# RMSNorm and projection: the rows of a triple loaded as quarters on four partition groups and turned by one VectorE transpose

## The chip, the cores and the metric

The kernel runs on one core of a Trainium2 chip. The metric is device time in microseconds, the median of three runs: 346.23 us for the kernel before (346.22 to 347.12). Engine names follow the profile: PE is TensorE (matmul), PEld its weight load, DVE is VectorE, ACT is ScalarE, POOL is GpSimd, SP is SyncE, which here only issues DMAs.

## The reference

```python
rms = np.sqrt(np.mean(x ** 2, axis=-1, keepdims=True) + eps)
x_norm = x / rms * gamma
return np.matmul(x_norm, w_qkv).astype(np.float32)
```

x is 8 x 1024 x 768 f32 (8192 rows), gamma 768, w_qkv 768 x 2304, the result 8192 x 2304 f32. The kernel needs x twice in different shapes: by rows for the mean of squares, and turned (the 768 inner elements on the partitions) as the left operand of the matmul.

## The kernel before

**Tiling.** The 8192 rows are 64 tiles of 128. The first seven are "plain" (PLAIN = 7): each is cast to bf16, turned by TensorE, multiplied by the bf16 weights `w_b` and scaled by its 1/rms while it leaves PSUM (`cast`, `stat`, `tr`, `cp`, `mm`, `evac`, `store`). They give TensorE work while w is loaded, multiplied by gamma (`conv`), bounded (`bound` to `scales`) and made into f16 operands (`unit`, `bsum`). The other 57 tiles are 19 "triples" of 384 rows. A triple times w is a block product of 3 row tiles x 2 halves of the inner dimension x 3 column thirds, done with 15 block products where the plain way has 18: 11 sums of x blocks (`sum_`, table ASUMS, on POOL, for triple 0 on VectorE too), 15 weight operands (six blocks and eleven combinations share the 15 slots, table BSUMS, made once), and 16 evacuations that combine partial results (`ev`, table VALUES: five plain ones on ACT, eleven with an addition on VectorE). One product (`prod`, matmul at L659) is three blocks of 128 by two column halves of 384: six matmuls. The inner index is split as k = 256 j + 2 m + two: "two" is the half, j = 0 to 2 the block, m the partition of the turned x.

**A triple's way in.** `load_t` (L599) loads 384 rows in one DMA into one of two buffers `xin`: partition p holds rows 3p to 3p+2, 9 KB in one piece. Three `tstat` (L607, ACT Square with an accumulator, 768 elements) give the sums of squares; `trms` (L611, ACT square root, 128x3) and `trecip` (L616, VectorE) make 1/rms. Three `tcast` (L450 through the helper `scaled`) write f16 rows times 1/rms into `xb`. Tile 0 is turned by three f32 TensorE transposes on f16 pairs seen as f32 (`ptr`, L503) and copied out of PSUM by ACT (`pcp`, L442); tiles 1 and 2 by two transposing DMAs from SBUF to SBUF (`pxbar`, L642, "the crossbar"). The turned triple stands in one of four slots of `xT`. `pstore` (L675) stores a third of a tile's columns, nine to a triple.

**The order.** It is written out by hand: the list PLAN names every operation once, and the kernel emits them in that order under `manual_schedule`, so that each engine's own order is that of the list. Each engine works in order, and a wait holds up what stands behind it on the same engine. The DMA queues are in order too: SP issues the loads of w and of the plain tiles, `load_t` 0 and 1, all stores and the crossbar transfers; ACT issues `load_t` 2 to 18 between its own instructions. Buffers: `xin` 2, `xb` 2, `xT` 4, `su` (the sums) 2, seven output buffers `outb`, nine more lent in `w_b` once w has been converted, and the eight PSUM banks in pairs. In the middle of the kernel the list reads, for TensorE, the preparation of x and the loads (evacuations, sums and stores left out):

```python
('prod', 8, 0, 1, 2), ('load_t', 11, 1, 'ACT'), ('trms', 10), ('prod', 8, 1, 1, 0), ('prod', 8, 2, 3, 4),
('prod', 8, 0, 2, 2), ('prod', 8, 1, 2, 0), ('prod', 8, 2, 4, 4), ('trecip', 10), ('tcast', 10, 0, 'p', 0, 'ACT'),
('prod', 8, 0, 3, 2), ('tcast', 10, 1, 'x', 0, 'ACT'), ('ptr', 10, 0, 6, 2), ('prod', 9, 2, 0, 0),
('tcast', 10, 2, 'x', 0, 'ACT'), ('pxbar', 10, 2, 1), ('prod', 9, 3, 0, 4), ('ev', 9, 'h2', 'P', 2)
```

Triple k uses `xin` buffer k mod 2 (the second argument of `load_t`), so `load_t` 11 writes over the rows of triple 9, and in ACT's order it stands behind the statistics of triple 10.

Of the kernel before, what the change touches and what calls it, by code (L numbers as in the profile page):

```python
# [38 lines left out]
    ('stat', 3), ('cp', 0, 'DVE', 1, 3), ('load_w', 9), ('load_w', 8), ('idle', 3, 0), ('tr', 3, 5), ('conv', 3, 3,
    'DVE'), ('prms', 3, 4), ('load_w', 10), ('precip', 3, 4), ('cp', 3, 'ACT'), ('mm', 0, 0, None, '3', 2), ('bound',  # L40
    0, 0, 'DVE'), ('load_x', 4, 4), ('cast', 1, 0, 'POOL', 0, 1), ('load_w', 12), ('stat', 1), ('mm', 3, 0, None, '0',
    6), ('load_w', 13), ('mm', 3, 0, None, '3', 6), ('conv', 4, 4, 'POOL'), ('load_w', 15), ('tr', 1, 0, 0, 1),
    ('cast', 1, 0, 'ACT', 1, 3), ('load_w', 14), ('cp', 1, 'ACT', 0, 1), ('idle', 1, 0), ('tr', 1, 1, 1, 3),
# [37 lines left out]
    None, '4', 0), ('tstat', 0, 2), ('mm', 4, 1, None, '2', 0), ('store', 3, 1), ('bsum', 't10', 1, 'DVE'), ('mm', 4,
    1, None, '3', 0), ('mm', 0, 2, None, '03', 2), ('tstat', 0, 0), ('bsum', 't4', 0, 'DVE'), ('mm', 0, 2, None, '14',
    2), ('bsum', 't5', 0, 'DVE'), ('trms', 0), ('mm', 0, 2, None, '25', 2), ('evac', 6, 1, 4, 'ACT'), ('trecip', 0),
    ('bsum', 't10', 0, 'DVE'), ('mm', 4, 1, None, '1', 0), ('mm', 4, 1, None, '5', 0), ('tcast', 0, 0, 'p', 0, 'ACT'),
    ('store', 6, 1), ('bsum', 't6', 0, 'DVE'), ('mm', 4, 2, None, '03', 4), ('evac', 0, 2, 5, 'ACT'), ('mm', 4, 2,
    None, '14', 4), ('tcast', 0, 1, 'x', 0, 'DVE'), ('mm', 4, 2, None, '25', 4), ('evac', 4, 1, 6, 'DVE'), ('unit',
    'b12', 1, 'ACT'), ('tcast', 0, 2, 'x', 0, 'POOL'), ('store', 0, 2), ('ptr', 0, 0, 2, 0), ('evac', 4, 2, 0, 'DVE'),
    ('mm', 1, 2, None, '03', 0), ('pcp', 0, 0, 'ACT'), ('pxbar', 0, 0, 2), ('mm', 1, 2, None, '14', 0), ('bsum', 't0',
    1, 'DVE'), ('tstat', 1, 1), ('mm', 2, 2, None, '03', 4), ('bsum', 't2', 0, 'DVE'), ('tstat', 1, 0), ('pxbar', 0,
    0, 1), ('mm', 2, 2, None, '25', 4), ('unit', 'b12', 0, 'DVE'), ('mm', 2, 2, None, '14', 4), ('tstat', 1, 2),  # L90
# [633 lines left out]
```

## Time and profile before

| | us |
|---|---|
| median of three runs | 346.23 |
| the profiled execution, its span | 344.0 |
| PE busy | 334.6 (97%) |
| DVE busy | 257.6 (75%) |
| ACT busy | 232.4 (68%) |
| POOL busy | 196.3 (57%) |
| all DMA: 115.61 MB | mean 336 GB/s |

The profile is of one execution. Its span runs from the first to the last instruction that it shows; the time of a run is taken on the device around the whole program and is 2.2 us longer. The parts of the page that are used below: the busy time of each engine; the span in 40 slices; the DMA queues with packets, megabytes and the share of the 16 DMA engines that their packets took; the groups of instructions by line, tile and shape, with count, busy time, mean ns of one, and the idle time of the engine ahead of them with what ended it; and the DMA issues with the median time from issue to landing. Of the trace's views, the windows give, for each stretch, its length and then for PE, PEld, DVE, ACT and POOL the busy us with the number of instructions, then the granted TensorE clock, the busy share of the DMA engines and GB/s; the timeline lists instructions with start, length, engine, line and the wait ahead; the view of one line gives shortest, median and longest ns and the first and the last start.

### The profile page before, as it was taken

How to read it: one execution, taken by the hardware profiler on the slowest of the kernel's cores; microseconds unless marked ns; L12 is line 12 of the kernel's file. 1: busy time of each engine (PE TensorE's matmuls, PEld its weight loads, DVE VectorE, ACT ScalarE, POOL GpSimd, SP SyncE). 2: the span in 40 equal slices, each digit the busy share in tenths (PEclk: the TensorE clock that was granted, in tenths of full speed). 3: DMA queues.
4: the chain of work that ended last, by engine and by line, in shares of the span. 5: the costliest groups of instructions: out<-in, count | busy, mean ns of one | idle time of the engine just before them, and what ended most of it. 6: DMA issues, size and time to landing. Idle time of an engine off the chain costs nothing. (4 is left out here: it accounts for less than half of the span.)

```text
span 344.0 us, 5987 instructions
## 1 busy us (share of the span) xinstructions
PE 334.6 (97%) x2078; PEld 202.2 (59%) x2078; DVE 257.6 (75%) x310; ACT 232.4 (68%) x354; POOL 196.3 (57%) x226
## 2 busy tenths in 40 slices
PE   7889999999999999999999999999999999999994
PEld 2556665666666666666666666666666666666662
DVE  3799999958677685957769595785959668596785
ACT  4589999578665849486684947768494778636310
POOL 1363114579394755929467492947739394891900
PEclk9999999999999999999999999999999999999998
DMA  7999999999999999999999999999999999977848
GB/s 266 402 398 417 404 303 326 309 359 320 321 380 326 392 305 363 305 333 382 286 397 297 361 336 326 395 299 387 302 344 365 318 393 311 374 299 219 339 174 312
DMA packets 64820, 115.61 MB, mean 336 GB/s; under 512 B 34195, under 2 KB 34710, under 8 KB 62358
## 3 DMA queue, kind: packets, MB, share of 16 engines
q1 hardware_dynamic: 62336, 95.18, 82.4%
q10 hardware_dynamic: 2454, 20.06, 18.1%
q8 instruction: 16, 0.26, 0.3%
q14 instruction: 14, 0.11, 0.1%
HBM read 32.25 MB, written 75.50 MB: 313 GB/s over the span
## 5 line engine op out<-in xcount | busy, mean ns | idle before, releaser
L659 PE MATMUL ps<-wq,su 128*128 128x384 f16 x1254 | 213.1, 326 | 0.0
L659 PEld LDWEIGHTS <-su 128*128 128x128 f16 x1254 | 122.7, 98 | 79.3
L455 POOL TENSOR_TENSOR su<-xT 128x384 f16<-128x384 f16 x73 | 64.6, 914 | 92.5 <-DMA xT<-xb 51.3
L672 DVE SCALAR_TENSOR_TENSOR outb<-ps,sc,pp 128x768 f32<-128x768 f32 (+1 forms) x83 | 82.2, 1001 | 18.3 <-PE ps L659 15.8
L659 PE MATMUL ps<-wq,xT 128*128 128x384 f16 x456 | 81.1, 326 | 0.0
L670 ACT ACTIVATE pp<-ps,sc 128x768 f32<-128x768 f32 x76 | 66.8, 904 | 14.4 <-PE ps L659 13.9
L672 DVE SCALAR_TENSOR_TENSOR pp<-ps,sc,pp 128x768 f32<-128x768 f32 x38 | 38.7, 1017 | 40.1 <-PE ps L659 39.9
L450 ACT ACTIVATE xb<-xin,rstd 128x768 f16<-128x768 f32 x53 | 48.7, 974 | 24.2 <-DVE rstd L616 24.1
L659 PEld LDWEIGHTS <-xT 128*128 128x128 f16 x456 | 44.6, 98 | 29.2
L672 DVE SCALAR_TENSOR_TENSOR w_b<-ps,sc,pp 128x768 f32<-128x768 f32 x51 | 51.6, 1015 | 2.3 <-ACT pp L670 0.6
L455 POOL TENSOR_TENSOR su<-su,xT 128x384 f16<-128x384 f16 x56 | 50.5, 925 | 4.7 <-DVE su L455 4.5
L670 ACT ACTIVATE outb<-ps,sc 128x768 f32<-128x768 f32 x19 | 17.1, 898 | 52.8 <-PE ps L659 52.8
L607 ACT ACTIVATE junk<-xin 128x768 bf16<-128x768 f32 x57 | 48.1, 844 | 0.6
L455 POOL TENSOR_TENSOR su<-su 128x384 f16<-128x384 f16 x38 | 35.4, 932 | 3.9 <-DVE su L455 1.0
L531 PE MATMUL ps<-w_b,su 128*128 128x384 bf16 x180 | 31.5, 326 | 1.9 <-DVE w_b L448 1.3
L455 POOL TENSOR_TENSOR su<-xT,su 128x384 f16<-128x384 f16 x36 | 32.3, 914 | 0.2
L531 PEld LDWEIGHTS <-su 128*128 128x128 bf16 x180 | 17.0, 98 | 14.0 <-issue 1.6
L672 DVE SCALAR_TENSOR_TENSOR w_b<-ps,sc,w_b 128x768 f32<-128x768 f32 x17 | 17.3, 1018 | 7.0 <-PE ps L659 5.1
L672 DVE SCALAR_TENSOR_TENSOR pp<-ps,sc,outb 128x768 f32<-128x768 f32 x19 | 19.3, 1016 | 0.6
L455 DVE TENSOR_TENSOR wq<-wq 128x1152 f16<-128x1152 f16 x22 | 18.6, 871 | 0.3
L442 ACT COPY xT<-ps 128x768 f16<-128x768 f16 (+1 forms) x20 | 15.8, 791 | 1.1 <-PE ps L503 1.0
L452 POOL TENSOR_SCALAR w_b<-wq,g_sb 128x768 bf16<-128x768 f32 x9 | 8.1, 905 | 7.9 <-DMA wq<-in_w_qkv_dram 6.6
(59 smaller groups left out, 151.8 us busy)
## 6 DMA issues: line engine op xcount, KB each, us to landing
out_dram<-outb SPq DMA_DIRECT2D x123, 384.0 KB, 6.2
out_dram<-w_b SPq DMA_DIRECT2D x68, 384.0 KB, 5.7
xin<-in_x_dram ACTq DMA_DIRECT2D x17, 1152.0 KB, 7.3
wq<-in_w_qkv_dram SPq DMA_DIRECT2D x14, 384.0 KB, 7.7
xin<-in_x_dram SPq DMA_DIRECT2D x2, 1152.0 KB, 11.9
pp<-in_x_dram SPq DMA_DIRECT2D x5, 384.0 KB, 7.5
wq<-in_w_qkv_dram SPq DMA_DIRECT2D x2, 768.0 KB, 9.2
xT<-xb SPq DMA_TRANSPOSE x38, 5.9
```

The source lines that it names most:

```text
L442: nc.scalar.copy(out=out, in_=in_)
L450: nc.scalar.activation(out=out, in_=in_, func=AF.Copy, scale=scale, bias=0.0)
L452: nc.gpsimd.tensor_scalar(out=out, in0=in_, scalar1=scale, scalar2=1.0, op0=mult, op1=mult)
L455: (nc.vector if eng == "DVE" else nc.gpsimd).tensor_tensor(out=out, in0=a, in1=b, op=op)
L531: nc.tensor.matmul(out=ps[:, b + hh, :CW], lhsT=XT[t][:, two, j, :], rhs=w_b[:, kb, n0:n0 + CW], start=(n == 1), stop=(n == KO), skip_grou ...
L607: nc.scalar.activation(out=junk[:, :K], in_=TX[k][:, i, :], func=AF.Square, accum_out=RS[k][:, i:i + 1])
L659: nc.tensor.matmul(out=ps[:, b + h, :CW], lhsT=left(k, a)[:, j, :], rhs=operand(w)[:, j, CW * h:CW * (h + 1)], start=(i == 0 and j == 0), ...
L670: nc.scalar.activation(out=o, in_=p, func=AF.Copy, scale=SC[sg], bias=0.0)
L672: nc.vector.scalar_tensor_tensor(out=o, in0=p, scalar=SC[sg], in1=q, op0=mult, op1=add if hs > 0 else sub)
```

## The change

x of a triple is loaded in another shape, and turned in another way.

- `load_t` takes the source as `"m (a q) -> a m q"`: partition 32a + r holds quarter a (192 elements, 768 B) of the rows 12r to 12r + 11. Each of a row's four quarters lies on another group of 32 partitions.
- `tstat` therefore has four instructions of 192 elements per tile where it had one of 768, and fills 12 columns of partial sums. A new `tsum` adds the four groups: one f32 matmul on TensorE with the constant `fold4` (128 x 128) and 12 columns, into PSUM. `trms` reads that from PSUM; `trms` and `trecip` work on 128 x 12.
- `tcast` has four instructions of 192 elements per tile.
- A new `tturn` turns a whole triple with one VectorE instruction: 32 x 32 blocks of f16 pairs seen as f32, 128 x 1152, from `xb` into `xT`. Which of the two halves an element belongs to is now the innermost index of `xT`, so the sums and the matmuls that read x itself take every other f16.
- `ptr`, `pcp`, `pxbar` and their helpers are gone: 57 turns on TensorE, 19 copies on ACT and 38 crossbar transfers.
- Since the order of the inner index on the partitions is now another, w is read with it: `"(a j c two) n -> a c j two n"`, and gamma and the partial loads and casts of the first plain tile likewise (`third`).
- PLAN is made anew. The counts of the other operations are the same. In the middle of the kernel it reads, cut as above:

```python
('prod', 8, 0, 1, 2), ('load_t', 11, 1, 'ACT'), ('prod', 8, 1, 1, 0), ('prod', 8, 2, 3, 4), ('prod', 8, 0, 2, 2),
('prod', 8, 1, 2, 0), ('tsum', 10, 6), ('trms', 10), ('prod', 8, 2, 4, 4), ('trecip', 10), ('tcast', 10, 0, 0, 'ACT'),
('prod', 8, 0, 3, 2), ('tcast', 10, 1, 0, 'ACT'), ('prod', 9, 2, 0, 0), ('tcast', 10, 2, 0, 'ACT'),
('tturn', 10, 1), ('prod', 9, 3, 0, 4), ('ev', 9, 'h2', 'P', 2)
```

The diff without PLAN, and without the lines that only drop the removed helpers:

```diff
     ctx.enter_context(tc.manual_schedule())
 
-    g3 = singles.tile([H, 2 * P], f32, name="g3")
-    nc.scalar.dma_start(out=g3, in_=gamma.rearrange("(j q) -> j q", q=2 * P))
+    Q = K // 4
+    g3 = singles.tile([H, 4, Q // H], f32, name="g3")
+    nc.scalar.dma_start(out=g3, in_=gamma.rearrange("(a j q) -> j a q", a=4, j=H))
     eps_sb = singles.tile([P, 1], f32, name="eps_sb")
     nc.vector.memset(eps_sb, float(eps))
...
     ident = singles.tile([P, P], bf16, name="ident")
     nc.vector.tensor_copy(out=ident, in_=ident_f)
-    ident_h = singles.tile([P, P], f16, name="ident_h")
-    nc.vector.tensor_copy(out=ident_h, in_=ident_f)
+    fold4 = singles.tile([P, 4, P // 4], f32, name="fold4")
+    nc.vector.tensor_reduce(out=fold4[:, 0, :], in_=ident_f.rearrange("p (a r) -> p r a", a=4), axis=mybir.AxisListType.X, op=add)
+    for a in range(1, 4):
+        nc.vector.tensor_copy(out=fold4[:, a, :], in_=fold4[:, 0, :])
     ones = singles.tile([1, P], bf16, name="ones")
     nc.gpsimd.memset(ones, 1.0)
...
     wq = singles.tile([P, 15 * H * C], f16, name="wq")
     w_b = singles.tile([P, KO, N], bf16, name="w_b")
-    xin = singles.tile([P, 2, 3, K], f32, name="xin")
+    xin = singles.tile([P, 2, 3 * K], f32, name="xin")
     pp = singles.tile([P, 7, C], f32, name="pp")
     xb = singles.tile([P, 2, 3 * K], f16, name="xb")
...
     zeros = nc.const_aps.tensor(0.0, [P, 1], f32).bitcast(bf16)[:, :1].to_broadcast([P, 512])
     wst = wq.bitcast(f32)
-    wv = w_qkv.rearrange("(j p two) n -> p j two n", p=P, two=2)
+    wv = w_qkv.rearrange("(a j c two) n -> a c j two n", a=4, j=H, two=2)
     lent = w_b.rearrange("p k n -> p (k n)").bitcast(f32)
     xbp = xb.rearrange("p a k -> p (a k)").bitcast(bf16)
...
             nc.tensor.matmul(out=ps[:, b, :], lhsT=zeros[:, :P], rhs=zeros, start=True, stop=True, skip_group_check=True)
 
+    def third(v, a, e):
+        return v.rearrange("p (g j q) -> p g j q", g=4, j=H)[:, :, a:e, :]
+
     def load_x(t, s, a=0, e=H):
         X[t] = pp[:, s, :]
-        nc.sync.dma_start(out=X[t][:, 2 * P * a:2 * P * e], in_=xf[t * P:(t + 1) * P, 2 * P * a:2 * P * e])
+        v = xf[t * P:(t + 1) * P, :]
+        if (a, e) == (0, H):
+            nc.sync.dma_start(out=X[t], in_=v)
+        else:
+            nc.sync.dma_start(out=third(X[t], a, e), in_=third(v, a, e))
 
     def load_w(i):
         twos, j, c, n0, n = PIECES[i]
         n1 = C * c + n0
-        nc.sync.dma_start(out=WF[i], in_=wv[:, j, twos[0]:twos[-1] + 1, n1:n1 + n])
+        nc.sync.dma_start(out=WF[i], in_=wv[:, :, j, twos[0]:twos[-1] + 1, n1:n1 + n])
 
     def gamma_in(b):
...
             two, j = divmod(kb, H)
             if j == 0:
-                nc.tensor.transpose(out=PT["g"][:, kb:kb + H], in_=g3[:, two::2], identity=ident_f[:H, :H])
+                nc.tensor.transpose(out=PT["g"][:, kb:kb + H], in_=g3.rearrange("j a q -> j (a q)")[:, two::2], identity=ident_f[:H, :H])
 
     def gamma_cp():
...
     def cast(t, s, eng, a=0, e=H):
         XB[t] = xbp[:, s * K:(s + 1) * K]
-        copy(eng, XB[t][:, 2 * P * a:2 * P * e], X[t][:, 2 * P * a:2 * P * e])
+        copy(eng, XB[t].rearrange("p (j g q) -> p g j q", g=4, j=H)[:, :, a:e, :], third(X[t], a, e))
 
     def stat(t):
...
 
     def load_t(k, s, eng="SP"):
-        TX[k] = xin[:, s, :, :]
+        TX[k] = xin[:, s, :]
         r0 = base + 3 * P * k
-        (nc.scalar if eng == "ACT" else nc.sync).dma_start(out=TX[k], in_=xf[r0:r0 + 3 * P, :].rearrange("(p i) k -> p i k", i=3))
+        (nc.scalar if eng == "ACT" else nc.sync).dma_start(out=TX[k], in_=xf[r0:r0 + 3 * P, :].rearrange("m (a q) -> a m q", a=4))
+
+    def rows(v, g, i):
+        return v[:, Q * (3 * g + i):Q * (3 * g + i + 1)]
 
     def tstat(k, i):
         if k not in RS:
-            RS[k] = stats.tile([P, 3], f32, name="ssq")
-        nc.scalar.activation(out=junk[:, :K], in_=TX[k][:, i, :], func=AF.Square, accum_out=RS[k][:, i:i + 1])
+            RS[k] = stats.tile([P, 12], f32, name="ssq")
+        for g in range(4):
+            n = 3 * g + i
+            nc.scalar.activation(out=junk[:, Q * (n % 8):Q * (n % 8 + 1)], in_=rows(TX[k], g, i), func=AF.Square, accum_out=RS[k][:, n:n + 1])
+
+    def tsum(k, b):
+        PT[k, "s"] = ps[:, b, :12]
+        nc.tensor.matmul(out=PT[k, "s"], lhsT=fold4.rearrange("p a r -> p (a r)"), rhs=RS[k], start=True, stop=True)
 
     def trms(k):
-        r = stats.tile([P, 3], f32, name="rms")
-        nc.scalar.activation(out=r, in_=RS[k], func=AF.Sqrt, scale=inv_k, bias=eps_sb)
+        r = stats.tile([P, 12], f32, name="rms")
+        nc.scalar.activation(out=r, in_=PT[k, "s"], func=AF.Sqrt, scale=inv_k, bias=eps_sb)
         RS[k] = r
 
     def trecip(k):
-        r = stats.tile([P, 3], f32, name="rstd")
+        r = stats.tile([P, 12], f32, name="rstd")
         nc.vector.reciprocal(out=r, in_=RS[k])
         RS[k] = r
 
-    def tcast(k, i, how, s, eng):
+    def tcast(k, i, s, eng, g0=0, g1=4):
         XBS[k] = s
-        TB[k, i] = xb[:, s, i * K:(i + 1) * K]
-        o, v = TB[k, i], TX[k][:, i, :]
-        if how == "x":
-            o = o.rearrange("p (two j m) -> p two j m", two=2, j=H)
-            v = v.rearrange("p (j m two) -> p two j m", two=2, j=H)
-        scaled(eng, o, v, RS[k][:, i:i + 1])
-
+        for g in range(g0, g1):
+            n = 3 * g + i
+            scaled(eng, rows(xb[:, s, :], g, i), rows(TX[k], g, i), RS[k][:, n:n + 1])
+
+    def tturn(k, s):
+        v = xb[:, XBS[k], :].bitcast(f32).rearrange("p (g b c) -> p g b c", g=4, c=P // 4)
+        o = xT[:, s, :].bitcast(f32).rearrange("p (b r g) -> p g b r", g=4, r=P // 4)
+        nc.vector.transpose(out=o, in_=v)
+        for i in range(3):
+            TT[k, i] = xT[:, s, i * K:(i + 1) * K].rearrange("p (j m two) -> p two j m", two=2, j=H)
 
     def left(k, a):
```

More of the change, by code (lines that the diff above doesn't have):

```diff
@@ L39 @@
[L39 to L43, printed above, removed]
@@ L81 @@
[L81 to L85, printed above, removed]
@@ L86 @@
[L86 to L90, printed above, removed]
@@ new lines @@
+    ('cp', 0, 'DVE', 0, 1), ('load_w', 6), ('idle', 1, 0), ('mm', 0, 0, None, '0', 2), ('cast', 0, 1, 'DVE', 1, 3), ('stat', 0),
+    ('load_w', 2), ('tr', 0, 4, 1, 3), ('load_w', 11), ('load_w', 5), ('cast', 3, 2, 'POOL'), ('stat', 3),
+    ('cp', 0, 'DVE', 1, 3), ('load_w', 9), ('load_w', 8), ('idle', 3, 0), ('tr', 3, 5), ('conv', 3, 3, 'DVE'), ('prms', 3, 4),
+    ('load_w', 10), ('precip', 3, 4), ('cp', 3, 'ACT'), ('mm', 0, 0, None, '3', 2), ('bound', 0, 0, 'DVE'), ('load_x', 4, 4),
+    ('cast', 1, 0, 'POOL', 0, 1), ('load_w', 12), ('stat', 1), ('mm', 3, 0, None, '0', 6), ('load_w', 13),
@@ new lines @@
+    ('mm', 3, 0, None, '3', 6), ('conv', 4, 4, 'POOL'), ('load_w', 15), ('tr', 1, 0, 0, 1), ('cast', 1, 0, 'ACT', 1, 3),
+    ('load_w', 14), ('cp', 1, 'ACT', 0, 1), ('idle', 1, 0), ('tr', 1, 1, 1, 3), ('load_x', 5, 5), ('conv', 1, 1, 'DVE'),
[8 rows of a table added]
+    ('evac', 1, 0, 0, 'DVE'), ('mm', 0, 0, None, '5', 2), ('conv', 8, 2, 'POOL'), ('evac', 0, 0, 1, 'ACT'),
+    ('evac', 2, 0, 2, 'DVE'), ('store', 1, 0), ('mm', 0, 1, None, '0', 4), ('mm', 0, 1, None, '2', 4), ('conv', 10, 4, 'POOL'),
+    ('bound', 1, 0, 'ACT'), ('store', 0, 0), ('mm', 0, 1, None, '5', 4), ('bound', 1, 2, 'DVE'), ('mm', 0, 1, None, '1', 4),
@@ new lines @@
+    ('store', 2, 0), ('mm', 1, 1, None, '0', 2), ('cast', 4, 4, 'POOL'), ('mm', 0, 1, None, '4', 4), ('mm', 1, 1, None, '2', 2),
+    ('bound', 1, 1, 'ACT'), ('tr', 4, 0), ('evac', 3, 0, 3, 'DVE'), ('mm', 1, 1, None, '3', 2), ('mm', 1, 1, None, '4', 2),
+    ('cp', 4, 'DVE'), ('mm', 1, 1, None, '5', 2), ('conv', 12, 0, 'POOL'), ('store', 3, 0), ('stat', 4),
+    ('mm', 1, 1, None, '1', 2), ('mm', 4, 0, None, '0', 6), ('evac', 1, 1, 4, 'DVE'), ('mm', 4, 0, None, '2', 6),
+    ('conv', 12, 3, 'POOL'), ('load_t', 1, 1), ('mm', 4, 0, None, '5', 6), ('prms', 4, 5), ('mm', 4, 0, None, '3', 6),
@@ new lines @@
+    ('precip', 4, 5), ('mm', 4, 0, None, '4', 6), ('bound', 2, 0, 'DVE'), ('store', 1, 1), ('conv', 13, 1, 'ACT'),
+    ('conv', 13, 4, 'POOL'), ('mm', 4, 0, None, '1', 6), ('mm', 0, 1, None, '3', 4), ('mm', 2, 1, None, '0', 0),
+    ('evac', 4, 0, 5, 'ACT'), ('conv', 15, 5, 'POOL'), ('mm', 2, 1, None, '4', 0), ('mm', 2, 1, None, '1', 0),
+    ('evac', 0, 1, 6, 'DVE'), ('bound', 2, 1, 'ACT'), ('mm', 2, 1, None, '3', 0), ('store', 4, 0), ('conv', 14, 2, 'POOL'),
+    ('mm', 2, 1, None, '2', 0), ('mm', 3, 1, None, '0', 2), ('bound', 2, 2, 1, 'DVE'), ('store', 0, 1),
@@ new lines @@
+    ('mm', 3, 1, None, '1', 2), ('cast', 5, 5, 'POOL'), ('mm', 3, 1, None, '4', 2), ('stat', 5), ('bound', 2, 2, 0, 'DVE'),
+    ('mm', 3, 1, None, '3', 2), ('mm', 2, 1, None, '5', 0), ('tr', 5, 6), ('stat', 6), ('fold',), ('cast', 6, 1, 'DVE'),
+    ('bound_tr', 7), ('mm', 3, 1, None, '2', 2), ('cp', 5, 'DVE'), ('tr', 6, 4), ('prms', 6, 7), ('bound_top',),
+    ('mm', 3, 1, None, '5', 2), ('prms', 5, 6), ('precip', 6, 7), ('bound_all', 5), ('cp', 6, 'ACT'),
+    ('mm', 5, 1, None, '0', 6), ('precip', 5, 6), ('scales',), ('mm', 5, 1, None, '2', 6), ('mm', 5, 1, None, '4', 6),
@@ new lines @@
+    ('trms', 0), ('bsum', 't2', 1, 'DVE'), ('trecip', 0), ('tstat', 1, 1), ('mm', 4, 1, None, '1', 0),
+    ('mm', 4, 1, None, '5', 0), ('tcast', 0, 2, 0, 'POOL'), ('evac', 4, 1, 6, 'DVE'), ('mm', 4, 2, None, '25', 4),
+    ('mm', 4, 2, None, '14', 4), ('mm', 4, 2, None, '03', 4), ('evac', 4, 2, 0, 'DVE'), ('unit', 'b11', 0, 'ACT'),
+    ('tcast', 0, 0, 0, 'ACT'), ('tcast', 0, 1, 0, 'POOL'), ('load_t', 2, 0, 'ACT'), ('evac', 5, 1, 1, 'ACT'), ('tstat', 1, 0),
+    ('bsum', 't10', 1, 'DVE'), ('evac', 0, 2, 5, 'ACT'), ('tstat', 1, 2), ('store', 0, 2), ('store', 4, 2),
[4 rows of a table added]
@@ new lines @@
+    ('store', 1, 2), ('bsum', 't6', 1, 'DVE'), ('unit', 'b12', 1, 'ACT'), ('evac', 5, 2, 4, 'ACT'), ('prod', 0, 3, 0, 0),
+    ('tsum', 1, 4), ('mm', 3, 2, None, '25', 2), ('sum', 0, 8, 0, 'POOL'), ('sum', 0, 1, 0, 'POOL'), ('trms', 1),
+    ('ev', 0, 'h0', 'P', 0), ('sum', 0, 0, 0, 'DVE'), ('sum', 0, 5, 0, 'DVE'), ('bsum', 't5', 0, 'DVE'),
+    ('bsum', 't6', 0, 'DVE'), ('bsum', 't0', 0, 'DVE'), ('prod', 0, 2, 0, 6), ('sum', 0, 4, 0, 'DVE'), ('bsum', 't1', 1, 'DVE'),
+    ('trecip', 1), ('tcast', 1, 0, 1, 'POOL'), ('tcast', 1, 1, 1, 'ACT'), ('bsum', 't0', 1, 'DVE'), ('bsum', 't7', 1, 'DVE'),
@@ new lines @@
+    ('ev', 0, 'h2', 'P', 2), ('sum', 0, 3, 0, 'DVE'), ('bsum', 't8', 1, 'DVE'), ('tcast', 1, 2, 1, 'ACT'), ('store', 2, 2),
+    ('store', 5, 1), ('store', 5, 2), ('tturn', 1, 1), ('mm', 6, 2, None, '03', 4), ('mm', 6, 2, None, '14', 4),
+    ('mm', 6, 2, None, '25', 4), ('sum', 1, 2, 1, 'POOL'), ('sum', 1, 3, 1, 'POOL'), ('sum', 1, 4, 1, 'POOL'), ('store', 4, 1),
+    ('prod', 0, 2, 1, 6), ('mm', 3, 2, None, '14', 2), ('prod', 0, 3, 1, 0), ('ev', 0, 'h3', 'P', 4), ('bsum', 't8', 0, 'DVE'),
+    ('sum', 1, 6, 1, 'POOL'), ('sum', 0, 9, 0, 'POOL'), ('sum', 1, 5, 1, 'POOL'), ('sum', 1, 0, 1, 'POOL'),
@@ L496, in precip, with turn @@
         nc.vector.reciprocal(out=rs_p[:, a:b], in_=rms_p[:, a:b])
[L498 to L504 removed]
+    def turn(src, bank, a=0, e=H):
         v = src.rearrange("p (j m two) -> p two j m", j=H, two=2)
[L506 removed]
+        o = ps[:, bank, :H * P].bitcast(bf16).rearrange("p (two j m) -> p two j m", j=H, two=2)
         for two in range(2):
             for j in range(a, e):
[L509 removed]
+                nc.tensor.transpose(out=o[:, two, j, :], in_=v[:, two, j, :], identity=ident)
         return o
     def tr(t, b, a=0, e=H):
[L513 removed]
+        PT[t, a] = turn(XB[t], b, a, e)
     def cp(t, eng, a=0, e=H):
```

499 lines of the change are left out of this document (228 added, 271 removed), and 83 rows, old and new, of the table PLAN.

## The prediction

> **What bounds the kernel now.** I read the page's head first, then the busy time by stage, then TensorE's timeline over one triple, then the DMA queues.
>
> ```profile
> span 344.0 us, 5987 instructions
> ...
> PE 334.6 (97%) x2078; PEld 202.2 (59%) x2078; DVE 257.6 (75%) x310; ACT 232.4 (68%) x354; POOL 196.3 (57%) x226
> ```
> ```profile
> 20.00:45.00 25.00, 25.00 (x167) 15.16 (x166) 23.97 (x40) 24.14 (x37) 9.00 (x10) 1.00 1.02 405
> ...
> 110.00:150.00 40.00, 40.00 (x250) 24.43 (x249) 28.73 (x33) 28.07 (x41) 27.41 (x32) 1.00 1.04 352
> ```
> ```profile
> 114.85 0.49 PE L503 MATMUL ps<-ident_f,xb 128*128 128x128 f32 x3
> 115.18 3.09 PE L659 MATMUL ps<-wq,su 128*128 128x384 f16 x18
> 118.10 3.09 PE L659 MATMUL ps<-wq,xT 128*128 128x384 f16 x18
> ...
> 129.88 0.55 PE L503 MATMUL ps<-ident_f,xb 128*128 128x128 f32 x3
> ```
>
> TensorE has no idle time in either stage. One triple lasts 129.88 - 114.85 = 15.03 us; 18 products' matmuls start within 118.10 - 115.18 = 2.92 us, so one matmul costs 0.162 us and the 90 of a triple 14.6 us. The three turns take the other 0.4 us. The last two columns of the stages are the DMA engines' mean busy share and GB/s: the 16 engines are as full as TensorE (1.04), and yet nothing waits for them for long enough to stop TensorE. So the kernel stands on two full resources, and a transfer that uses the 16 engines unevenly must be looked at first.
>
> ```profile
> q1 hardware_dynamic: 62336, 95.18, 82.4%
> q10 hardware_dynamic: 2454, 20.06, 18.1%
> ```
> ```profile
> out_dram<-outb SPq DMA_DIRECT2D x123, 384.0 KB, 6.2
> out_dram<-w_b SPq DMA_DIRECT2D x68, 384.0 KB, 5.7
> xin<-in_x_dram ACTq DMA_DIRECT2D x17, 1152.0 KB, 7.3
> wq<-in_w_qkv_dram SPq DMA_DIRECT2D x14, 384.0 KB, 7.7
> xin<-in_x_dram SPq DMA_DIRECT2D x2, 1152.0 KB, 11.9
> ...
> wq<-in_w_qkv_dram SPq DMA_DIRECT2D x2, 768.0 KB, 9.2
> xT<-xb SPq DMA_TRANSPOSE x38, 5.9
> ...
> g<-in_gamma_dram ACTq DMA_DIRECT2D x1, 3.0 KB
> ```
>
> q10 is ACT's queue (packets, MB, share of 16 engines). Its packets can be counted out: 17 loads of 128 rows are 2176 packets of 9 KB, and 278 are left. 278 = 17 x 16 + 6: each triple's load closes with one packet on each of 16 engines, and gamma, three rows of 1 KB, has three data packets and **three** closing ones. A transfer whose outermost count is 3 ran on three engines; its rows weren't cut to fill more. Every other load of before has 128 or 256 outermost, and ran on 16.
>
> **The change part by part.** *The loads* decide it. The sources are written with the quarter first: `"m (a q) -> a m q"` for a triple, `"(a j c two) n -> a c j two n"` for w. As built, a triple's source is 4 x 384 runs of 192 elements (768 B), a piece of w 4 x 32 rows (4 x 64 for the two double ones); the SBUF side keeps 128 partitions. By the count above these 35 transfers can be cut four ways: I take **four engines** for them, while the 191 stores and the loads of plain tiles stay on 16.
>
> The Trainium skill, "DMA: Bandwidth & Descriptors", section "Why a DMA increments its semaphore by 16 and not by 1", gives the rule behind the row: the descriptor generator takes the slowest dimension that isn't 1 on each side and uses the largest k up to 16 that divides both. For 4 against 128 that is 4. By that rule the trace agrees: gamma's 3. The row alone leaves a second reading, that the partitions count (gamma has 3 of those too); that reading is rival B, and by the page it is out.
>
> Rates, per engine: the stage from 20 to 45 us moves 405 / 16 = 25.3 GB/s; q10 moves 20.06 MB in 0.181 x 16 x 344 = 996 engine-us, 20.1 GB/s, beside the stores. No row has 768 B packets. The far end is the crossbar's 256 B packets: q1's 0.824 x 16 x 344 = 4535 engine-us, less 87.7 MB at 25.3 (3466), leave 1069 for 38 x 768 packets, 36.6 ns each, 26.5 over their bytes; 768 B would so take 57 ns, 13.5 GB/s. I take 20.1, the row of the same transfer. Then, on each of the four engines: a triple's load 1.18 MB / 4 / 20.1 = 14.7 us (11.7 at 25.3, 21.9 at 13.5); a store 0.393 MB / 16 / 25.3 = 0.97 us, nine of a triple 8.7 us. **23.4 us of DMA for a triple that TensorE does in 15.0.** w is 7.08 MB / 4 / 25.3 = 70 us, where it was hidden in the first 25.
>
> *The start.*
> ```profile
> L468 SPq DMA_DIRECT2D wq<-in_w_qkv_dram x16: 328/376/661, 0.7 to 17.2; - x16
> ```
> ```profile
> L559 DVE TENSOR_REDUCE bmax<-bnd x1: 167/167/167, 29.5 to 29.5; 128x1 bf16<-128x10 f32 x1
> ```
> ```profile
> L659 PE MATMUL ps<-wq,su x1254: 325/326/326, 55.4 to 338.8; 128*128 128x384 f16 x180
> ```
> ```profile
> L607 ACT ACTIVATE junk<-xin x57: 830/843/867, 36.6 to 300.9; 128x768 bf16<-128x768 f32 x57
> ```
> The last piece of w is issued at 17.2 and lands near 25; the largest |w| follows at 29.5, the first product at 55.4, 26 us later, which TensorE spends on plain tiles in an order that doesn't change much. With four engines w lands at about 0.7 + 2 + 70 + 7 (seven x tiles, on all 16) = 80, so the first product isn't before 109. The x of triples 0 and 1 come behind w on SP: 80 + 2 x 14.7 + 7 early stores = 116; and in ACT's new order a statistic of triple 1 stands ahead of the first scaling of triple 0, so triple 0's product waits for that too: **118** with scaling and turn, against 55.4.
>
> *The triples.* 17 loads are left (2 to 18). ACT issues each, in order, behind statistics of the triple before, whose x must have landed. In triples 2 to 8 the order lets a load be issued while the one before it still moves, so the engines set the pace, 20 to 24 us; in 9 to 15 each load stands directly behind the last statistic of the one before: 14.7 + 2 of latency + 6 for the stores that fall into it + 5 of statistics = 28. I take 24 for all 17: 408 us. From the last statistic (300.9) to the end before are 43 us, with no load left in them. **118 + 408 + 43 = 569 us of span.** The median of the runs, 346.2, is 2.2 us over the span; so 571, and I say 570.
>
> *Everything else* is inside these waits if I am right, and counts only in the rivals:
>
> ```profile
> L450 ACT ACTIVATE xb<-xin,rstd 128x768 f16<-128x768 f32 x53 | 48.7, 974 | 24.2 <-DVE rstd L616 24.1
> L607 ACT ACTIVATE junk<-xin 128x768 bf16<-128x768 f32 x57 | 48.1, 844 | 0.6
> ...
> L442 ACT COPY xT<-ps 128x768 f16<-128x768 f16 x19 | 15.0, 791 | 1.0 <-PE ps L503 1.0
> ...
> L607 ACT ACTIVATION_READ_ACCUMULATOR junk<-xin 128x1 f32 x57 | 11.2, 197 | 0.0
> ...
> L611 ACT ACTIVATE rms<-ssq,eps_sb 128x3 f32<-128x3 f32 x19 | 5.6, 296 | 0.6
> ...
> L450 ACT ACTIVATE wq<-w_b,inv 128x1152 f16<-128x1152 bf16 x4 | 4.9, 1247 | 0.0
> ```
> ```profile
> 128.90 2.74 ACT L450 ACTIVATE xb<-xin,rstd 128x768 f16<-128x768 f32 x3 [1.89 <-DVE rstd L616]
> 131.52 0.90 ACT L670 ACTIVATE pp<-ps,sc 128x768 f32<-128x768 f32 x1
> ```
> A scaling of 768 elements becomes four of 192. From 974 to 1247 ns are 384 elements, 0.71 to 0.81 ns each; three elements take 296. So 192 take about 0.45 us, 0.36 with the 0.1 that neighbours overlap (3 x 0.974 in 2.74): 12 are 4.3 us where three took 2.7. The statistics go from 3 x 0.96 to 12 x 0.4 to 0.5, each with its own accumulator read. ACT then has 13.3 to 14.5 us of work in a triple: it fits, barely, since the 0.8 copy goes. VectorE gains one turn of 1152 elements; no row has one; 0.67 (a 1152-element add) to 3 us, 1.5 taken, in a gap of 2.6 us that it has before the triple's first combination. TensorE loses 19 x 0.4 and gains 19 folds of 12 columns (0.2 to 0.5, 0.3 taken). POOL's sums now read every other f16: 0.91 us each, up to 1.4 if that costs, and 11 fit into 23 us either way. The 38 crossbar transfers free 67 us of each engine: no use to the four that are full.
>
> **The rivals.**
> B, *all 16 engines carry the loads* (partitions count). For it: gamma's row can be read so. Against: then a 4 x 384 source must be cut within its quarters, which no transfer here shows. Then ACT's chain decides. The fold is queued on TensorE behind the 13th product; root, reciprocal and all 12 scalings follow, and ACT's order has the next triple's first evacuation (h2) behind them, for which the 4th product of its chain waits: about 1.0 (matmul, root, reciprocal) + 4.3 + 0.9 = 6.2 us, with five products and the fold, 5.2 us, to hide it. 1.0 us of stall in 15 of the 18 passages: 344 - 7.6 + 5.7 + 15 + 2 (ACT full from 20 to 45) + 2.2 = **361**.
> C, *faster*: 16 engines, and a scaling of 192 elements takes 0.28 us or less, so that chain is covered. Against: the 296 ns of three elements. 344 - 7.6 + 19 x 0.2 + 2.2 = **342**.
> D, inside my case: T is 20.4 (25.3 GB/s): 114 + 347 + 43 + 2 = **506**, or 480 if the engines overlap packets better still; or 30.6 (13.5 GB/s): 118 + 520 + 43 + 2 = **683**.
>
> **How the numbers follow.** Four engines 0.85, B 0.10, C 0.04, something else 0.01. The 0.85 rests on gamma's three closing packets beside sixteen for each other load. My range is 480 to 690, the ends of D; I give it 0.95 of the four-engine case, 0.81 in all. Faster by over 0.3% (about what a measurement here can tell) is C, 0.04; within 0.3% 0.01; slower 0.95.
>
> **What would show it.** The first x load of a triple landing in over 14 us instead of 7.3 and w's last piece near 80 us; closing packets of ACT's queue 17 x 4; a DMA share near 0.5 to 0.7 with TensorE idle in every triple behind the fold, and the fold behind ACT's statistics, and these behind the DMA of xin. If xin lands in about 7 us and w by 26, I am wrong at the first step, and the 4th product's wait for h2 tells B from C.

## The result

The changed kernel takes **688.94 us** (685.68 to 694.38, four runs) against 346.23 before; the ratio is 1.989 (95% interval 1.979 to 1.999). The forecast was 570, with 480 to 690 as its range: slower for the reason that it gave, but 119 us longer, 1 us inside the far end. Two of the four runs (691.14 and 694.38) lie beyond that end.

The page of the changed kernel, its head and its DMA queues (packets, MB, share of 16 engines):

```profile
span 684.9 us, 6334 instructions
...
PE 392.7 (57%) x2059; PEld 217.0 (32%) x2059; DVE 302.6 (44%) x330; ACT 278.5 (41%) x840; POOL 201.3 (29%) x236
...
q1 hardware_dynamic: 36072, 87.70, 34.6%
q10 hardware_dynamic: 26195, 20.06, 12.4%
```

The queue of ACT now carries 17 x 1536 = 26112 packets of 768 B for the triples. 83 are left: 12 data packets and 3 closing ones of gamma, and 68 = 17 x 4. Each load closes on **four** engines. The 16 together are busy for only 47% of the span (both large queues), because the other twelve have the stores and the plain tiles alone.

The groups of the page that wait longest (count, busy us, mean ns, then idle us ahead of the group and what ended it):

```profile
L643 PE MATMUL ps<-wq,su 128*128 128x384 f16 x1254 | 241.4, 353 | 141.8 <-ACT pp L654 124.8
...
L441 POOL TENSOR_TENSOR su<-xT 128x384 f16<-128x384 f16 x73 | 66.0, 922 | 339.4 <-DVE xT L624 339.4
L599 ACT ACTIVATE junk<-xin 128x192 bf16<-128x192 f32 x228 | 79.4, 350 | 187.6 <-DMA xin<-in_x_dram 187.2
```

TensorE waits for ACT's evacuations, but ACT itself waits 187 us for x: the statistics of the next triple stand in ACT's order between two evacuations. ("Fold" below is the matmul of `tsum`.) One passage on ACT's timeline and on TensorE's (start, length, and in brackets the idle time ahead):

```profile
396.30 0.36 ACT L599 ACTIVATE junk<-xin 128x192 bf16<-128x192 f32 x1 [14.88 <-DMA xin<-in_x_dram]
...
397.70 0.88 ACT L654 ACTIVATE pp<-ps,sc 128x768 f32<-128x768 f32 x1
...
400.02 0.55 ACTq L589 DMA_DIRECT2D xin<-in_x_dram  x1
...
408.00 4.26 ACT L436 ACTIVATE xb<-xin,rstd 128x192 f16<-128x192 f32 x12 [0.30 <-DVE rstd L612]
412.16 2.46 ACT L654 ACTIVATE pp<-ps,sc 128x768 f32<-128x768 f32 x3
429.44 0.36 ACT L599 ACTIVATE junk<-xin 128x192 bf16<-128x192 f32 x1 [14.83 <-DMA xin<-in_x_dram]
...
433.16 0.56 ACTq L589 DMA_DIRECT2D xin<-in_x_dram  x1
```
```profile
398.63 8.64 PE L643 MATMUL ps<-wq,su 128*128 128x384 f16 x36 [14.67 <-ACT pp L654]
...
413.09 3.08 PE L643 MATMUL ps<-wq,xT 128*128 128x384 f16 x18 [0.81 <-ACT pp L654]
```

The loop can be read off: a load is issued at 400.02, its x is there at 429.44 (29.4 us), 3.7 us of statistics (with an evacuation among them) follow, and only then, at 433.16, the next load is issued: 33.1 us a triple, of which TensorE works some 18. The view of the load's line and of w's (shortest, median and longest issue in ns, first and last start) gives the mean over all 17 and the start:

```profile
L589 ACTq DMA_DIRECT2D xin<-in_x_dram x17: 551/564/11615, 132.6 to 609.9; - x17
```
```profile
L461 SPq DMA_DIRECT2D wq<-in_w_qkv_dram x16: 530/3400/8143, 0.7 to 66.4; - x16
```
```profile
L643 PE MATMUL ps<-wq,su x1254: 322/326/528, 139.4 to 679.7; 128*128 128x384 f16 x180
```

(609.9 - 132.6) / 16 = 29.8 us from load to load; w's last piece is issued at 66.4 where it was 17.2, and the first product starts at 139.4 where it was 55.4.

### The profile page after: what moved, and what is told of

Its sections match the earlier page's. It is cut to its first block, busy times and chain, and to the rows that moved or that the text cites. A ratio compares the mean times of both kernels' runs of the same rounds, so it can differ in the third digit from the quotient of the medians.

```text
span 684.9 us, 6334 instructions
## 1 busy us (share of the span) xinstructions
PE 392.7 (57%) x2059; PEld 217.0 (32%) x2059; DVE 302.6 (44%) x330; ACT 278.5 (41%) x840; POOL 201.3 (29%) x236
## 5 line engine op out<-in xcount | busy, mean ns | idle before, releaser
L643 PE MATMUL ps<-wq,su 128*128 128x384 f16 x1254 | 241.4, 353 | 141.8 <-ACT pp L654 124.8
L643 PEld LDWEIGHTS <-su 128*128 128x128 f16 x1254 | 131.1, 105 | 246.4 <-issue 176.7
L599 ACT ACTIVATE junk<-xin 128x192 bf16<-128x192 f32 x228 | 79.4, 350 | 187.6 <-DMA xin<-in_x_dram 187.2
L643 PE MATMUL ps<-wq,xT 128*128 128x384 f16 x456 | 90.3, 349 | 38.6 <-ACT pp L654 37.7
L436 ACT ACTIVATE xb<-xin,rstd 128x192 f16<-128x192 f32 x216 | 77.2, 441 | 7.7 <-DVE rstd L612 7.7
L518 PE MATMUL ps<-w_b,su 128*128 128x384 bf16 x180 | 43.7, 404 | 26.6 <-DVE w_b L434 17.1
L624 DVE STREAM_TRANSPOSE xT<-xb 128x1152 f32<-128x1152 f32 x19 | 43.8, 2304 | 20.9 <-ACT xb L436 20.8
L599 ACT ACTIVATION_READ_ACCUMULATOR junk<-xin 128x1 f32 x228 | 42.9, 188 | 0.0
L603 PE MATMUL ps<-ssq,fold 128*128 128x12 f32 x38 | 6.9, 255 | 43.1 <-ACT junk L599 32.0
L612 DVE RECIPROCAL rstd<-rms 128x12 f32<-128x12 f32 x19 | 4.3, 226 | 54.7 <-ACT rms L607 54.7
```

Source lines behind the costliest of these rows:

```text
L436: nc.scalar.activation(out=out, in_=in_, func=AF.Copy, scale=scale, bias=0.0)
L518: nc.tensor.matmul(out=ps[:, b + hh, :CW], lhsT=XT[t][:, two, j, :], rhs=w_b[:, kb, n0:n0 + CW], start=(n == 1), stop=(n == KO), skip_grou ...
L599: nc.scalar.activation(out=junk[:, Q * (n % 8):Q * (n % 8 + 1)], in_=rows(TX[k], g, i), func=AF.Square, accum_out=RS[k][:, n:n + 1])
L603: nc.tensor.matmul(out=PT[k, "s"], lhsT=fold4.rearrange("p a r -> p (a r)"), rhs=RS[k], start=True, stop=True)
L612: nc.vector.reciprocal(out=r, in_=RS[k])
L624: nc.vector.transpose(out=o, in_=v)
```

## Experiments

Theory 1 is the forecast's: an outermost count of four confines a load to four engines. Theory 2 puts it on the small packets, theory 3 on the new computation. e2, e3, e4, e6 and e8 were run once, the others four times. In the diffs the fronts of some lines are left out.

**e1, every load on 16 engines.** A load is cut into four DMAs by quarter, so that its outermost count is 384 or 32. All else is the changed kernel.

```diff
-    dma_start(out=TX[k], in_=xf[r0:r0 + 3 * P, :].rearrange("m (a q) -> a m q", a=4))
+    for a in range(4):
+        dma_start(out=TX[k][32 * a:32 * a + 32, :].rearrange("r (i q) -> r i q", q=Q),
+                  in_=xf[r0:r0 + 3 * P, Q * a:Q * (a + 1)].rearrange("(r i) q -> r i q", i=12))
...
-    dma_start(out=WF[i], in_=wv[:, :, j, twos[0]:twos[-1] + 1, n1:n1 + n])
+    for a in range(4):
+        dma_start(out=WF[i][32 * a:32 * a + 32], in_=wv[a, :, j, twos[0]:twos[-1] + 1, n1:n1 + n])
```

> The changed kernel with every load of w and of a triple's x issued as four DMAs, one for each group of 32 partitions (outermost counts 384 or 32 where there were 4); packets, order and all computation as in the changed kernel. Theory 1 (four engines carry the loads, and that is all of the loss): 1536 packets of 52 ns over 16 engines are 5.0 us, so xin lands within 10 us, TensorE stops only about 0.8 to 1.0 us a triple for h2, and the time is 355 to 370 us. Theory 2 (768 B packets are slow on any engines): a load stays over 20 us and the time over 600. Theory 3 (ACT's new chain of statistics, fold, root and scalings holds the kernel by itself): loads land fast and the time stays over 400.

Measured 410.41 us (ratio 1.182, 1.178 to 1.186). ACT's queue has 27215 packets, 26112 + 15 + 17 x 4 x **16**:

```profile
q10 hardware_dynamic: 27215, 20.06, 24.1%
```

278.5 of the 342.7 us that were lost come back with nothing changed but the number of DMAs and their engines. Theory 2 falls (the packets are the same), and so does "that is all of the loss": 64 us remain, the time is over the 355 to 370 expected, and theory 3's sign for this run, over 400, came true. e5 decides between them.

**e2 and e3, one half each**: only the x loads, or only w's, as in e1.

> Only the x loads of the triples as four DMAs, w's loads as in the changed kernel. Theory 1: w's last packet stays at 73 us, the first product comes about 30 us behind it (103 against 139), then the triples run at their own pace: 361 + 103 - 55 = about 405 us, 395 to 420. Theory 2: over 600. Theory 3: over 450.

> Only w's loads as four DMAs, the triples' loads as in the changed kernel. Theory 1: w has landed by 35 us, the loads of triples 0 and 1 take some 20 us each behind it, the first product comes at 80 to 90 us instead of 139, and the 17 loads keep their 30 us each: 687 - 55 = about 632 us, 615 to 650. Theory 2: the same, since the triples' packets are unchanged. Theory 3: the same.

Measured 454.68 and 641.0. w on four engines costs 44 us beside e1, where 103 - 55 = 48 was expected; the level of e2 was missed (395 to 420), since its base of 361 was some 50 too low, and it too lies where theory 3 had it. e3 is as expected, and the triples' loads cost 231 beside e1.

**e4, four engines without the rest of the change**, on the kernel before:

```diff
-    in_=xf[r0:r0 + 3 * P, :].rearrange("(p i) k -> p i k", i=3)
+    in_=xf[r0:r0 + 3 * P, :].rearrange("(a r i) k -> r a (i k)", r=4, i=3)
```

> The kernel before, with one edit: a triple's load takes its rows in another order (partition 32r + a gets row group 4a + r), so that the source's outermost count is 4 while packets stay 9 KB; the rows of a triple come out permuted in the output, all else is the same work. Theory 1: four engines, 1.18 MB / 4 / 20 GB/s = 14.7 us of load and 8.7 us of stores on them in a triple, so 23 to 25 us a triple: 75 + 17 x 24 + 43 = about 526 us, 470 to 560. Theory 2 (small packets are what is slow): about 350 us. Theory 3: about 347, since none of the new ACT work is in it.

Measured 605.55, over the expected 470 to 560. Packets of 9 KB and none of the new computation, and the time is still 1.75 times that of the kernel before. The load's line and its queue (17 x 128 packets, 17 x 4 closing ones, gamma's 6):

```profile
L602 ACTq DMA_DIRECT2D xin<-in_x_dram x17: 536/537/653, 70.6 to 533.0; - x17
```
```profile
q10 hardware_dynamic: 2250, 20.06, 10.7%
```

28.9 us from load to load, more than the 24 expected: theory 1 is right, its size too small here too. The expectation left out the crossbar transfers, which are still in this kernel: by the prediction's 67 us for all 19 triples they are 3.5 us of each engine in a triple. With the load itself (0.107 x 16 x 603.8 us over 17 loads and four engines, 15.2) and the 8.7 of stores that makes 27.4 us of work for each of the four.

**e8, two engines**: e3 with a load as two DMAs of outermost count 2 (`"m (a q) -> a m q", a=2` on each half of the columns).

> e3_w16 with a triple's load as two DMAs whose sources have an outermost count of 2 (halves a = 0, 1 and a = 2, 3, 64 partitions each, packets of 768 B). Theory 1 (the outermost count is the number of engines, and each DMA takes the same first ones): two engines carry a load, 768 packets x 52 ns = 40 us and 9.3 us of stores on each, 50 to 55 us a triple with 4 us of statistics: about 80 + 17 x 54 + 43 = 1040 us, 950 to 1150. Rival (engines go by partitions, or two DMAs take four engines): 630 to 650, as e3_w16.

Measured 974.68, within the expected range.

```profile
q10 hardware_dynamic: 26195, 20.06, 8.6%
```
```profile
L592 ACTq DMA_DIRECT2D xin<-in_x_dram x34: 525/13779/20069, 120.8 to 893.7; - x34
```

34 DMAs close with 68 packets, two each, and a load comes every 48 us ((893.7 - 120.8) / 16). Had the two DMAs of a load run on different engines, it would have gone as in e3. So 16, 4 and 2 engines give 410, 641 and 975 us with w's loads repaired. The Trainium skill, "DMA: Bandwidth & Descriptors", section "Why a DMA increments its semaphore by 16 and not by 1", says that a DMA on k engines has the lowest-numbered k. That the two DMAs of a load share their engines fits this; which engines they are, no run here shows.

**e5, the computation alone**: the changed kernel with the loads of before.

```diff
-    in_=xf[r0:r0 + 3 * P, :].rearrange("m (a q) -> a m q", a=4)
+    in_=xf[r0:r0 + 3 * P, :].rearrange("(p i) k -> p (i k)", i=3)
...
-    wv = w_qkv.rearrange("(a j c two) n -> a c j two n", a=4, j=H, two=2)
+    wv = w_qkv.rearrange("(j p two) n -> p j two n", p=P, two=2)
...
-    dma_start(out=WF[i], in_=wv[:, :, j, twos[0]:twos[-1] + 1, n1:n1 + n])
+    dma_start(out=WF[i], in_=wv[:, j, twos[0]:twos[-1] + 1, n1:n1 + n])
```

> The changed kernel's computation and order with the loads of w and of the triples as the kernel before has them (one DMA each, 3 KB and 9 KB packets, 16 engines). The data then lie on the wrong partitions, so the output is not the reference's; every instruction is the changed kernel's but for the sources of 35 DMAs. Theory 1 (the 64 us that the repaired loads of e1_xw16 leave over the kernel before are mostly the loads themselves: four times as many DMAs for SP to issue at the start, 768 B packets): 355 to 370 us, with a stop of 0.8 us a triple for h2 and no other. Rival (they are the new computation and order): 395 to 410.

Measured 373.04 (ratio 1.075, 1.071 to 1.079), 3 us over theory 1's range and far from the rival's: 26 us are the new computation and order, so theory 3 doesn't carry e1's 410 and e2's 455 either. TensorE's timeline in the regular passages:

```profile
238.83 0.29 PE L603 MATMUL ps<-ssq,fold 128*128 128x12 f32 x2
...
244.81 3.09 PE L643 MATMUL ps<-wq,xT 128*128 128x384 f16 x18 [0.81 <-ACT pp L654]
247.73 6.99 PE L643 MATMUL ps<-wq,su 128*128 128x384 f16 x42
254.56 0.29 PE L603 MATMUL ps<-ssq,fold 128*128 128x12 f32 x2
```

254.56 - 238.83 = 15.73 us a passage, with the one stop for h2, 0.81 us. The forecast's rival B had that at 1.0. In the kernel before most passages of this stretch take 14.95 (turns at 144.89, 159.84, 174.79; the prediction's 15.03 is one of the longer ones). The nine passages from the 8th fold to the 17th (159.93 to 302.01, against 144.89 to 279.46 before) cost 7.5 us. Of the 28 us by which the span is longer, 15 lie ahead of them, between the first fold and the 8th, where the order is irregular and VectorE nearly full (26.3 of the 30 us from 55 to 85): the first two folds that stand among products are 78.01 - 56.82 = 21.2 us apart, with 20 matmuls of plain tiles (3.3 us) and two long stops between them. The other 5 lie behind the 17th. These 20 us were not taken apart further.

```profile
56.82 0.29 PE L603 MATMUL ps<-ssq,fold 128*128 128x12 f32 x2
...
62.50 1.14 PE L643 MATMUL ps<-wq,xT 128*128 128x384 f16 x6 [1.64 <-ACT pp L654]
...
71.44 6.73 PE L643 MATMUL ps<-wq,su 128*128 128x384 f16 x30 [2.21 <-DVE su L441]
78.01 0.29 PE L603 MATMUL ps<-ssq,fold 128*128 128x12 f32 x2
```

**e7, h2 earlier**: e1 with `('ev', k - 1, 'h2', ...)` ahead of `('tcast', k, 2, ...)` in PLAN for k = 8 to 14.

> e1_xw16 with one thing moved: in triples 8 to 14 the first evacuation h2 of the triple before stands ahead of the last four scalings in ACT's order, not behind them. Theory (the 4th product waits 0.81 us for h2 because 12 scalings stand ahead of it): the stop goes in those seven passages, 410 - 7 x 0.8 = about 404 us; the turn comes 0.9 us later, which POOL's sums still cover. Rival (h2 is only the last of several waits, the turn or the sums come next): 408 to 412.

Measured 413.29 (1.191, 1.185 to 1.198): no gain. The rival had it, 1 us under the time and not with the waits it named:

```profile
241.97 2.11 PE L656 MATMUL ps<-wq,xT 128*128 128x384 f16 x12 [0.50 <-ACT pp L667]
244.37 6.99 PE L656 MATMUL ps<-wq,su 128*128 128x384 f16 x42 [0.29 <-DVE pp L669]
```

One stop has become two of about the same sum. They wait for an evacuation of ACT and one of VectorE; that these now stand behind the last scalings and the turn is read from the order, not tried by itself.

**e9, less on ACT**: e5 with the third tile's scalings on POOL, behind its sums, for k = 8 to 14.

> e5_compute with the last four scalings of a triple on POOL (behind its sums of the triple before) and not on ACT, in triples 8 to 14. In e5_compute a passage of these triples takes 15.73 us where TensorE alone needs 14.9, and TensorE stops 0.81 us for h2. Theory (ACT's 12 scalings ahead of three evacuations are the stop): POOL's four at 0.58 us run beside ACT's eight, ACT is free 1.4 us sooner, the passages take 14.9 to 15.0 us, and the time falls by 7 x 0.8 = 5.6 us, 373 to about 367.5. Rival (POOL is late, the turn then holds the sums and the products): passages of 15.5 us or more, 371 or above.

Measured 366.39 (1.058, 1.054 to 1.062), 6.6 less than e5:

```profile
249.87 1.63 POOL L449 TENSOR_SCALAR xb<-xin,rstd 128x192 f16<-128x192 f32 x4
```
```profile
248.39 0.29 PE L614 MATMUL ps<-ssq,fold 128*128 128x12 f32 x2
248.53 1.14 PE L654 MATMUL ps<-wq,xT 128*128 128x384 f16 x6
249.50 4.06 PE L654 MATMUL ps<-wq,su 128*128 128x384 f16 x24
253.40 3.09 PE L654 MATMUL ps<-wq,xT 128*128 128x384 f16 x18
256.32 6.99 PE L654 MATMUL ps<-wq,su 128*128 128x384 f16 x42
263.15 0.29 PE L614 MATMUL ps<-ssq,fold 128*128 128x12 f32 x2
```

No stop is left, and a passage takes 14.76 us, below the 14.95 of the kernel before: the amount of work on ACT ahead of the evacuations was the wait, and the one other order that was tried (e7, on e1's loads) did not mend it.

**e10, e6, e11 and e12, the load that four DMAs leave.** e10 is e5 with e1's x loads; e6 and e11 put four DMAs a load into the kernel before, with 768 B and with 9 KB packets; e12 is e10 with all 76 of them issued by SP (`nc.sync.dma_start` for both cases of `eng`).

> e5_compute with the triples' loads as in e1_xw16 (four DMAs of 768 B packets on 16 engines) and w's loads still as before; the output is not the reference's, as in e5_compute. It parts the 37 us between e5_compute (373) and e1_xw16 (410). Theory (the x loads' packets cost here what they cost the kernel before in e6_before_x768, 23 us, and w's 64 DMAs the other 14, as the first product's start does, 78 against 56): about 392 to 398 us. Rival (all of it is w at the start): 373 to 378.

> The kernel before with a triple's load as four DMAs of 768 B packets on 16 engines; the data lie on the wrong partitions, so the output is not the reference's. It adds to the kernel before what e1_xw16 keeps of the changed x loads, with the crossbar transfers still there. A packet of 768 B took 60 ns in e1_xw16 where 9 KB took 450: 12 x 60 = 720, so a load costs each engine 2.2 us more, and the engines were full. Theory 1 (packets and DMA count are the residual): 365 to 385 us. Rival (the residual is computation): 346 to 352.

> The kernel before with a triple's load as four DMAs of 32 partitions each, packets still 9 KB on 16 engines, the output the reference's. It parts the 23 us of e6_before_x768 into packets and number of DMAs. Theory (the packets): 346 to 350 us. Rival (57 more DMA issues on ACT's and SP's queues): 360 to 372.

> e10_compute_x16 with the triples' 76 load DMAs issued by SP and none by ACT; nothing else is changed, and the output is not the reference's, as there. In e10 the 68 issues on ACT's sequencer take 49.1 us in all, where the 17 of e5_compute took 5.9, and in the worst passage ACT stands 4.7 us behind them. Theory (the 24 us between e5 and e10 are ACT held by issuing): SP carries the issues, and the time falls to 375 to 382 us. Rival (they are the packets on the DMA engines, whoever issues them, or the loads wait behind stores on SP's queue): 390 us or above.

Measured: e10 396.91 (1.146, 1.141 to 1.151), e6 369.96, e11 360.0 (1.039, 1.032 to 1.045), e12 377.31 (1.086, 1.082 to 1.091). So x in four DMAs costs 24 us in the new kernel and 23 in the old, and w's 64 DMAs the other 13.5 of e1. My theory for e11, that the packets were all of the price, fell: four DMAs of 9 KB packets cost 13.4 us alone, and the small packets the other 10 of e6. Three rows, the x issues of e5, of e10 and of e12:

```profile
L589 ACTq DMA_DIRECT2D xin<-in_x_dram x17: 334/335/365, 49.4 to 307.2; - x17
```
```profile
L590 ACTq DMA_DIRECT2D xin<-in_x_dram x68: 567/628/1892, 55.5 to 331.7; - x68
```
```profile
L590 SPq DMA_DIRECT2D xin<-in_x_dram x76: 560/616/1792, 21.4 to 312.8; - x76
```

In e10 an issue takes 0.63 us and there are 68; its worst passage shows what stands behind them on ACT:

```profile
326.13 1.74 ACTq L590 DMA_DIRECT2D xin<-in_x_dram  x2
326.79 0.88 ACT L655 ACTIVATE pp<-ps,sc 128x768 f32<-128x768 f32 x1
327.91 4.33 ACTq L590 DMA_DIRECT2D xin<-in_x_dram  x2
332.36 0.36 ACT L600 ACTIVATE junk<-xin 128x192 bf16<-128x192 f32 x1 [4.69 <-DMA xin<-in_x_dram]
```

ACT does nothing until the fourth issue is out. Here 3.07 of the 4.33 us are not the issuing itself: the program's DMAs take eight completion semaphores in turn, the fourth issue has that of the first (100 in the trace), and it begins 0.02 us after that DMA has landed. It is the only such wait of ACT's in e10; otherwise the 68 issues' own 49.1 us hold it. Moved to SP, the same DMAs with the same packets cost 4 us over e5, not 24: 20 of them go with the issuing on ACT. (e12's loads also start at other times, since nothing of ACT's stands ahead of them; the two were not parted.)

e11's 13.4 us have another wait beside them. Its issues on ACT take only 0.32 us, but 32 of the 68 begin 0.02 us after an earlier DMA with the same semaphore has landed, most often a store or a crossbar transfer, and ACT's sequencer stands 36 us for them in all. The view of waits shows it ahead of ACT's roots, which read nothing of a store:

```profile
ACT rms L613 <- DMA out_dram<-w_b: 29.4, 9, 5.2
```

No run here shows how much of the 13.4 us this is.

## Why the prediction was right, and where it was not

- **Four engines: right**, by the closing packets (68 and not 272), by e1 (278.5 us back), by e4 (this alone takes the kernel before to 605.55) and by e8 (two engines).
- **The rate: wrong, and the largest miss.** "I take 20.1, the row of the same transfer" was a row of 9 KB packets. From the page, 0.124 x 16 x 684.9 = 1359 us for 26112 packets are 52 ns each, 14.8 GB/s, near the 13.5 that was worked out from the 256 B packets and kept only as an end. A load is then 26112 / 17 x 52 ns / 4 = 20 us of each of the four engines, not 14.7, and with the 8.7 of stores a triple is 28.7, not 23.4.
- **"I take 24 for all 17": wrong, mostly by the same rate.** It was 29.8. From the load of triple 2 to that of 9 (132.62 to 332.97) it was 28.6 each, where the engines set the pace as the text had it, and their sum is now 28.7. From 9 to 15 each load stands directly behind the last statistic of the one before, and it was 32.6; the text's 28 with 5.3 us more of packets is 33. Its own weights, 23.4 and 28, would have made 25 and not 24; the rate is the far larger part. 17 x 5.8 us is some 98 of the 116 us of span that were missing (569 against 684.9).

```profile
332.97 0.56 ACTq L589 DMA_DIRECT2D xin<-in_x_dram  x1
```
```profile
528.64 0.56 ACTq L589 DMA_DIRECT2D xin<-in_x_dram  x1
```

- **The range held the result partly by luck.** Its end, 683, came from the 256 B packets' price, 57 ns, and kept the start at 118, though two early loads of 21.9 us instead of 14.7 would have added 14. With the 52 ns that were measured its sum is 118 + 17 x 28.7 + 43 + 2 = 651; the start's 21 us and the 18 by which the chained loads raise the mean, neither of them in that sum, take it to the end of the range.
- **The path to TensorE: in part another.** The stops were foretold at the fold. Ahead of the fold TensorE stood 43.1 us; ahead of the products it stood 162.5 us for ACT's evacuations (124.8 and 37.7), which stand in ACT's order behind the same statistics and the same loads. What starts the chain, the DMA of `xin`, is as foretold.
- **118 for the first product: too early**, it was 139.4, and by a wait that the sum did not have. w was about right: the largest |w| follows at 89.8 where 80 + 4.5 was forecast. But the early stores go through SP's queue behind the two x loads and in part through the same four engines. Behind the load of triple 0 four stores take 25 us to issue (the first of them 22.75 alone), so that triple 1's load is issued only at 103.24, and the store behind that one takes 16. ACT twice stands before the evacuation of a plain tile whose output buffer is not yet stored, until 106.5 and until 126.8; triple 1's statistics, triple 0's scaling, its turn and the rest of the plain tiles' matmuls all come after. The sum had put these stores in as seven times 0.97 us.

```profile
L546 DVE TENSOR_REDUCE bmax<-bnd x1: 166/166/166, 89.8 to 89.8; 128x1 bf16<-128x10 f32 x1
```
```profile
78.16 25.03 SPq L530 DMA_DIRECT2D out_dram<-outb  x4
103.24 0.56 SPq L589 DMA_DIRECT2D xin<-in_x_dram  x1
103.89 16.15 SPq L530 DMA_DIRECT2D out_dram<-outb  x1
```
```profile
106.54 1.88 ACT L436 ACTIVATE outb<-ps,rs_p 128x768 f32<-128x768 f32 x2 [11.89 <-DMA out_dram<-outb]
...
126.78 0.90 ACT L436 ACTIVATE outb<-ps,rs_p 128x768 f32<-128x768 f32 x1 [11.50 <-DMA out_dram<-outb]
```

- **43 for the end: about right**, 684.9 - 645.3 = 39.6 from the last statistic:

```profile
L599 ACT ACTIVATE junk<-xin x228: 345/348/363, 108.3 to 645.3; 128x192 bf16<-128x192 f32 x114
```

- **The new operations: mostly right**: 12 scalings in 4.26 us (4.3 forecast), the fold 0.29 (0.3), POOL's sums 0.92 with every other f16 (0.91 before). Statistics took 0.35 us (0.4 to 0.5), the turn took 2.30 (1.5 taken, 3 its bound):

```profile
L624 DVE STREAM_TRANSPOSE xT<-xb 128x1152 f32<-128x1152 f32 x19 | 43.8, 2304 | 20.9 <-ACT xb L436 20.8
```

- **Rival B's 361 did not come**: with 16 engines and the loads of before it was 373, for the irregular triples at the start above all; the h2 stop was there, at 0.81 for 1.0. And 16 engines are not to be had in one DMA of this layout as the kernel writes it; in four they cost 37 us more (e1 against e5). No version here beats the kernel before; e9's passages of 14.76 us say that the computation could in its regular part, by 0.2 us a triple; the loads that it needs could not, as tried here.

## What to carry to other kernels

Before costing a new access pattern, read off its outermost count on both sides and count the closing packets of a transfer like it: here the engines that carry it came first, the packet size second. Price a transfer by the packet size that it will have, and if a load is issued behind the work on the load before, count the whole loop (issue, landing, work) and not the transfer alone. When a load has to be cut into several DMAs, ask which engine issues them, and whether an issue waits for an earlier DMA's semaphore: here the same DMAs cost 24 us on ACT and 4 on SP.

## What the runs showed of the hardware

- **TensorE is slower after a long stop.** After the 14.67 us above, 36 matmuls took 8.64 us, at a granted clock of 0.50 from 398.6 to 402 us and of 0.80 from 402 to 407; in e1, after 0.24 us, 6.01 at a clock of 1.00 (247 to 255). The longest in a group is 528 ns against a median of 326, and the granted clock of the span 0.782. The Trainium skill, "TensorE: Matmul & The Clock Gate", Part 1, tells of a clock that idle windows halve; the trace agrees. PE is busy for 392.7 us here and for 340.7 in e5, which has the same instructions and a granted clock of 0.995. That is not what made the kernel slow: in the passage above the loop of load and statistics does not run through TensorE.

```profile
248.39 6.01 PE L645 MATMUL ps<-wq,su 128*128 128x384 f16 x36 [0.24 <-ACT pp L656]
```

- **An issue is not of fixed length.** One triple's load took 0.33 us to issue as 128 rows (kernel before) and 0.55 as 4 x 384 runs, and four of the 17 took 5.6 to 11.6 us, issued while another load was still moving; a piece of w took 0.38 on 16 engines and 3.4 on four (medians).
